# Inverse of the DeltaNet chunk matrix: masks applied to the decay factors, the diagonal written ahead of the row operations, one group of 64-row matmuls queued later

## Chip, cores and metric

The kernel runs on one core of one Trainium2 chip. The metric is the device time of one execution in microseconds, taken as the median of several runs. A core has TensorE (PE, with weight loads listed apart as PEld), VectorE (DVE), ScalarE (ACT), GpSimd (POOL) and SyncE (SP). Each works through its own queue in order. DMAs are started from the queues of SP and ACT here, and an engine that has to start a DMA waits at that place of its queue until the DMA's input is ready.

## What is computed

The reference is one layer of a hybrid decoder with 512 tokens, 16 meta tokens and a width of 2048: one input projection, three token mixers side by side (gated DeltaNet with 6 heads, gated linear attention (GLA) with 5, forgetting attention with 5), gates, and one output projection. The change concerns the DeltaNet mixer. In chunks it solves a unit lower triangular system for each head:

```
decay = exp(where(causal, g[..., :, None] - g[..., None, :], -inf))
a_mat = where(strict, einsum('bhncd,bhnsd->bhncs', kb, kc) * decay, 0.0)
sol   = triangular_solve(eye + a_mat, rhs, lower=True, unit_diagonal=True)
```

The kernel uses chunks of 128 tokens (and one of the 16 meta tokens) and computes the inverse of `eye + a_mat` explicitly.

## The kernel before

**The projection carries the time line.** The input projection is a long run of matmuls (line 174, tile `pp`): 128x128 weight blocks in two parts each (`whi` and `wlo`, so that the product is nearly exact) against the normalised input. A weight half of 128x1024 is loaded by SP, rounded to `whi` by ACT (L144), and the rest `wlo` is formed by DVE (L145). There are two buffers of each, so the cast of a half waits until PE has done with the half before the last one. A head's columns take 48 matmuls of 512 columns or 96 of about 264. Everything else (DeltaNet, GLA, attention) is put in between these matmuls by a scheduler that orders each engine's queue when the program is built. The list `order` holds the projection's matmuls as they are traced. `behind(mm, n)` makes a matmul follow the n-th projection matmul traced after that point; with `PM = (308,310)` it holds back the first 32-row matmul of each group's inverse.

**DeltaNet runs in two groups of three heads.** For a group, `dn_keys` makes the keys (projection, convolution, SiLU), then for the meta tokens and for each of the four 128-token blocks: the transposed keys `pk`, the key products `pg` (L433), the decay differences `e2` on DVE (L434) clamped at zero from below, their exponential on ACT (L435), and the product `an = pg * scale * e2` on DVE (L438). Below the diagonal `an` holds the negated matrix; on and above the diagonal it holds other finite values, because the clamp makes the decay factor 1 there. A POOL select (L412) is already in use for another tile of the same shape, `at`.

`dn_inverse` then works in four steps.

1. The 32x32 diagonal blocks of `an` (48 of them, and three 16x16 of the meta tokens) are written to DRAM (`scr`, L449, and `scmeta`, L453) and read back as 51 rows of 1024 (`ab`, L454 and L455), all from ACT's queue. `ab` is zeroed first by POOL (L446).
2. Thirty pairs of DVE operations (L463 and L465) turn each row into the inverse by row operations. They stand in DVE's queue between weight splits and evacuations.
3. Two POOL selects (L466 and L468) put zeros above the diagonal and ones on it. Then `ab` goes to DRAM (`sc`, L471) and comes back as `xc` and `xm` (L474, L476, tiles `iv` and `xm`). DVE transposes them (L478, L479).
4. From the 32-row inverses come the 64-row and 128-row ones: matmuls `pm` (L485), ACT copies (L489), matmuls `pl` (L494, L495), an ACT copy (L496), copies into `uf` (ACT L502, DVE L504), and for each half q the matmuls `pn` (L515), an ACT copy (L517), matmuls `pu` (L520) and a DVE copy (L521). `uf` is zeroed by POOL (L499).

`dn_mix` then runs the recurrence with `uf`. The order in which the parts are traced is: keys, values, queries, inverse, mixing of group 0, the same for group 1, then the GLA gates (`gz`, `stgz`, `zsgz`), GLA pairs (`gk`, ...), and attention. SiLU takes a maximum on POOL (L294), three ACT steps (L295 to L297) and a product on DVE (L298).

Of the kernel before, what the change touches and what calls it, by code (L numbers as in the profile page):

```python
# [14 lines left out]
ALU = mybir.AluOpType  # L15
# [12 lines left out]
H = 3  # L28
# [49 lines left out]
def tile_hybrid_trunk(ctx, tc, xT, xtok, mtok, w_gate, w_in, w_out, consts, lmask, fin_w, out, dbg=None):  # L78
# [20 lines left out]
    V, A, G, PE = nc.vector, nc.scalar, nc.gpsimd, nc.tensor  # L99
# [62 lines left out]
    def behind(mm, n):  # L162

        later.append((mm.ins, len(order) + n))
# [85 lines left out]
    for b in range(5):  # L250
        r = NM if b == 4 else P
# [9 lines left out]
    for b in range(5):  # L261
        r = NM if b == 4 else P
# [55 lines left out]
    for k in range(KT):  # L318
        for xx in (xh, xl):
            for a in range(2):  # L320
                PE.matmul(pgate[a][:, :HT], wg[k // 8][:, k % 8, :], xx[k][:, a * HT : (a + 1) * HT],
                          start=(k == 0 and xx is xh), stop=(k == KT - 1 and xx is xl))
# [35 lines left out]
    def conv_silu(key, blk, dst, meta=True):  # L358

        t0 = 0 if meta else NM  # L360
        pb = row(f"pb{blk}")
        if meta:
            G.memset(pb[:, 0:3], 0.0)
        evac(inproj(key, first=0 if meta else NM - 4), pb, off=3)
        c = row(f"cv{blk}")[:, t0:T]
        V.tensor_scalar_mul(c, pb[:, t0:T], cwc[:, blk, 0:1])
        for w in range(1, 4):
            V.scalar_tensor_tensor(out=c, in0=pb[:, t0 + w : w + T], scalar=cwc[:, blk, w : w + 1], in1=c,  # L368
                                   op0=ALU.mult, op1=ALU.add)
        silu(dst[:, t0:], c, f"c{blk}")  # L370
# [4 lines left out]
    def dn_keys(g):  # L375

        st = {}
        hs = range(H * g, H * g + H)
        kT = six.tile([P, H, T], F32, tag="six", name=f"kT{g}")
        for j, h in enumerate(hs):  # L380
            conv_silu(("dk", h), 6 + h, kT[:, j])
        gb = six.tile([P, H, T], F32, tag="six", name=f"gb{g}")
        nc.scalar.dma_start(out=gb, in_=gd[6 + H * g : 6 + H * g + H, :].partition_broadcast(P))
        kd = six.tile([P, NN, P], F32, tag="six", name=f"kd{g}")
        at = six.tile([P, NN, P], F32, tag="six", name=f"at{g}")
        an = six.tile([P, NN, P], F32, tag="six", name=f"an{g}")
        sk = wk.tile([P, 5, H], F32, tag="sk", name=f"sk{g}")
        kdm = t15(f"kdm{g}", (NM, H, P))
        anm = wk.tile([NM, H, NM], F32, tag="anm", bufs=1, name=f"anm{g}")
        atm = wk.tile([NM, H, NM], F32, tag="atm", bufs=1, name=f"atm{g}")  # L390
        cols = wk.tile([P, 4, 5, H], F32, tag="cols", name=f"cols{g}")
        nb2, br, nbg, tmp = (cols[:, i] for i in range(4))
        gcl = lambda b, j: gcol[:NM if b == 4 else P, b, 6 + H * g + j : 6 + H * g + j + 1]
        G.memset(sk, 1.0)
        for b in (4, 0, 1, 2, 3):
            r = NM if b == 4 else P
            ts = slice(0, NM) if b == 4 else bsl(b)
            pk = psm.tile([P, 512], F32, tag="m", name=f"pk{g}{b}")
            for j in range(H):
                PE.transpose(pk[:r, j * P : (j + 1) * P], kT[:, j, ts], ident)  # L400
            for j in range(H):
                sq = wk.tile([P, P], BF16, tag="sq", name=f"sqk{g}{b}{j}")
                A.activation(sq[:r], pk[:r, j * P : (j + 1) * P], AF.Square, accum_out=sk[:r, b, j : j + 1])
            e = at[:, b * H : b * H + H, :] if b < 4 else atm
            for j in range(H):
                V.tensor_scalar(e[:r, j, :], gb[:r, j, ts], gcl(b, j), 0.0, ALU.subtract, ALU.min)
            A.activation(e, e, AF.Exp)
            for j in range(H):
                dst = kd[:, b * H + j, :] if b < 4 else kdm[:, j, :]
                V.tensor_scalar_mul(dst, pk[:r, j * P : (j + 1) * P], e[:r, j, r - 1 : r])  # L410
            if b < 4:
                G.affine_select(out=e, in_=e, pattern=[[0, H], [1, P]], base=0, channel_multiplier=-1,  # L412
                                compare_op=ALU.is_ge, fill=0.0)
        A.activation(tmp, sk, AF.Ln, bias=eps_c)
        A.activation(br, tmp, AF.Exp, scale=-0.5)
        lb = gcol[:, :, H * g : H * g + H]
        gg = gcol[:, :, 6 + H * g : 6 + H * g + H]
        for sl, r in ((slice(0, 4), P), (slice(4, 5), NM)):
            c = lambda t: t[:r, sl, :]
            A.activation(c(tmp), c(lb), AF.Exp)  # L420
            V.tensor_tensor(out=c(nb2), in0=c(tmp), in1=c(br), op=ALU.mult)
            V.scalar_tensor_tensor(out=c(tmp), in0=c(nb2), scalar=-1.0, in1=c(br), op0=ALU.mult, op1=ALU.mult)
            V.tensor_copy(c(br), c(nb2))
            V.tensor_copy(c(nb2), c(tmp))
            A.activation(c(nbg), c(gg), AF.Exp)
            V.tensor_tensor(out=c(nbg), in0=c(nbg), in1=c(nb2), op=ALU.mult)
        for b in (4, 0, 1, 2, 3):
            r = NM if b == 4 else P
            ts = slice(0, NM) if b == 4 else bsl(b)
            pg = psm.tile([P, 512], F32, tag="m", name=f"pg{g}{b}")  # L430
            e2 = t15(f"e2{g}{b}")
            for j in range(H):
                PE.matmul(pg[:r, j * r : (j + 1) * r], kT[:, j, ts], kT[:, j, ts], start=True, stop=True)  # L433
                V.tensor_scalar(e2[:r, j, :r], gb[:r, j, ts], gcl(b, j), 0.0, ALU.subtract, ALU.max)  # L434
            A.activation(e2[:r, :, :r], e2[:r, :, :r], AF.Exp, scale=-1.0)  # L435
            for j in range(H):
                dst = an[:, b * H + j, :] if b < 4 else anm[:, j, :]
                V.scalar_tensor_tensor(out=dst, in0=pg[:r, j * r : (j + 1) * r], scalar=nb2[:r, b, j : j + 1],  # L438
                                       in1=e2[:r, j, :r], op0=ALU.mult, op1=ALU.mult)
        st.update(kT=kT, kd=kd, at=at, an=an, kdm=kdm, anm=anm, br=br, nbg=nbg)  # L440
        return st

    def dn_inverse(g, st):
        an, anm = st["an"], st["anm"]
        ab = six.tile([NN * 4 + H, 1024], F32, tag="six", name=f"ab{g}")
        G.memset(ab, 0.0)  # L446
        scr = drp.tile([NN * 4, 1024], F32, tag="scr", name=f"scr{g}", bufs=2)
        for r in range(4):
            nc.scalar.dma_start(  # L449
                out=scr.rearrange("(n r) (a c) -> r a n c", r=4, a=32)[r],  # L450
                in_=an[32 * r : 32 * r + 32, :, 32 * r : 32 * r + 32])
# [3 lines left out]
        nc.scalar.dma_start(  # L455
            out=ab[NN * 4 : NN * 4 + H, :].rearrange("h (a c) -> h a c", a=32)[:, 0:NM, 0:NM],
            in_=scm_.rearrange("a h c -> h a c"))
        a3 = ab.rearrange("p (a c) -> p a c", a=32)
        for j in range(1, 31):
            m = 31 - j  # L460
# [2 lines left out]
            V.tensor_tensor(out=t3, in0=a3[:, j + 1 :, j : j + 1].to_broadcast([NN * 4 + H, m, j]),  # L463
                            in1=a3[:, j : j + 1, 0:j].to_broadcast([NN * 4 + H, m, j]), op=ALU.mult)
            V.tensor_tensor(out=a3[:, j + 1 :, 0:j], in0=a3[:, j + 1 :, 0:j], in1=t3, op=ALU.add)  # L465
        G.affine_select(out=a3, in_=a3, pattern=[[1, 32], [-1, 32]], base=0, channel_multiplier=0,  # L466
                        compare_op=ALU.is_gt, fill=0.0)
        G.affine_select(out=a3, in_=a3, pattern=[[1, 32], [-1, 32]], base=0, channel_multiplier=0,  # L468
                        compare_op=ALU.not_equal, fill=1.0)
        sc2 = drp.tile([NN * 4 + H, 1024], F32, tag="sc2", name=f"sc2{g}", bufs=2)  # L470
        nc.scalar.dma_start(out=sc2, in_=ab)  # L471
        iv = six.tile([P, 4, NN, 32], F32, tag="six", name=f"iv{g}")
# [9 lines left out]
        for n in range(NN):  # L482
            for q in range(2):
                lo_, hi_ = slice(64 * q, 64 * q + 32), slice(64 * q + 32, 64 * q + 64)
                mm = PE.matmul(pm[lo_, n, :], an[hi_, n, lo_], uc[hi_, n, :], start=True, stop=True)  # L485
# [12 lines left out]
        uf = six.tile([P, NN, P], F32, tag="six", name=f"uf{g}")  # L498
# [6 lines left out]
        for q in range(2):  # L505
            ns = range(q * 6, q * 6 + 6)
            nsl = slice(q * 6, q * 6 + 6)
            b64 = t15(f"b64{g}{q}", (64, 6, 64))
            G.memset(b64, 0.0)
            V.tensor_copy(b64[0:32, :, 0:32], xc[0:32, nsl])  # L510
            V.tensor_copy(b64[32:64, :, 32:64], xc[32:64, nsl])
            V.tensor_copy(b64[32:64, :, 0:32], l1[32:64, nsl])
            pn = psm.tile([64, 6, 64], F32, tag="m", name=f"pn{g}{q}")
            for n in ns:
                PE.matmul(pn[:, n - q * 6, :], an[64:128, n, 0:64], uf[64:128, n, 64:128], start=True, stop=True)  # L515
            m2 = t15(f"m2{g}{q}", (64, 6, 64))
            A.copy(m2, pn)  # L517
            pu = psm.tile([64, 6, 64], F32, tag="m", name=f"pu{g}{q}")
            for n in ns:
                PE.matmul(pu[:, n - q * 6, :], b64[:, n - q * 6, :], m2[:, n - q * 6, :], start=True, stop=True)  # L520
            V.tensor_copy(uf[0:64, q * 6 : q * 6 + 6, 64:128], pu)  # L521
# [362 lines left out]
    PM = (308,310)  # L884
# [85 lines left out]
    for cc in range(4):  # L970
# [7 lines left out]
        n = (FIRST // 2, KT // 2, KT // 2, LAST // 2)[cc]  # L978
# [27 lines left out]
    for tb in range(4):  # L1006
# [9 lines left out]
        r = rr[:, tb : tb + 1]  # L1016
# [67 lines left out]
```

## Time and profile before

| what | value |
|---|---|
| runs | 1031.01, 1032.09, 1033.81 us; median 1032.09 |
| profiled execution | 1035.39 us, span 1033.7 us, mean granted TensorE clock 0.992 |
| PE busy | 1011.4 us, 7799 matmuls |
| row operations L463 / L465 | 60 each, 20.1 / 21.4 us |
| selects L466 / L468 | 2 each, mean 1258 / 1404 ns |
| selects L412 (128x384) | 8, mean 1175 ns |
| `sc` to `iv`, issue to issue | 208.49 to 215.15 us in group 0, 392.80 to 399.48 us in group 1 |

"Busy" counts an engine's instructions as they run; a wait in the list of waits is time in which the engine's queue stood still until the named instruction of another engine was done. The granted clock is the share of TensorE's full clock in a stretch. A line of the timeline gives the start in us from the span's start, the duration, engine, line, operation, tile written and tiles read, sizes, and how many instructions were merged; in brackets the idle time ahead of it and what ended it.

### The profile page before, as it was taken

To read this page: it belongs to the slowest core of one execution; us is meant where nothing else is said; L and a number is where in the kernel's file an instruction comes from. 1 tells how busy PE (TensorE), PEld (TensorE's weight loads), DVE (VectorE), ACT (ScalarE), POOL (GpSimd) and SP (SyncE) were. 2 spreads that over 40 slices of the span, in tenths; PEclk is the share of its full clock that TensorE was granted. 3 is DMA by queue.
4 is the path that set the end of the run, shared out by engine and by line. 5 is a ranking of instruction groups with operands and counts; after the bars stand their busy time and mean duration, and the time that the engine had idled before them with its cause. 6 is when DMAs were issued, how large, how long until landed. Compare 5 with 4: busy or idle time off the path is not lost.

```text
span 1033.7 us, 19032 instructions
## 1 busy us (share of the span) xinstructions
PE 1011.4 (98%) x7799; PEld 910.3 (88%) x7799; DVE 566.7 (55%) x1240; ACT 411.7 (40%) x899; POOL 136.4 (13%) x137
## 2 busy tenths in 40 slices
PE   9999999999999998999989999999999999999996
PEld 7899999989999888899989879898998988888885
DVE  6366868856577883243747474445454574423234
ACT  6644533343455343243444444343333353213223
POOL 0022212221122222100101010110101010000014
PEclk9999999999999998999999999999999999999998
DMA  9613232323222233132112122222232254222244
GB/s 354 239 62 115 83 90 91 102 78 108 78 83 81 78 102 99 49 94 74 62 48 83 44 92 66 91 82 92 82 93 82 93 193 133 82 100 85 102 142 163
DMA packets 42347, 105.15 MB, mean 102 GB/s; under 512 B 10589, under 2 KB 13917, under 8 KB 42260
## 3 DMA queue, kind: packets, MB, share of 16 engines
q1 hardware_dynamic: 28000, 92.33, 26.3%
q10 hardware_dynamic: 14260, 11.61, 4.1%
q8 instruction: 61, 1.00, 0.4%
q14 instruction: 26, 0.21, 0.1%
HBM read 98.74 MB, written 5.05 MB: 100 GB/s over the span
## 4 chain that ended last, share of the span: by engine, by line
PE 66%; DVE 5%; DMA 3%; issue 3%; ACT 2%; POOL 1%; ACTq 0%; POOLq 0%; DVEq 0%
PE pp L174 39%; PE pa L932 15%; DMA sc<-ab 1%; PE pss L717 1%; POOL stgz L294 1%; DVE wlo L145 1%; PE pfo L877 1%; PE pfa L845 1%; PE py L593 1%; PE pb L932 1%; PE pfx L860 1%; DVE ab L465 1%; PE po L608 1%; PE po L607 1%; PE pa L570 0%
## 5 line engine op out<-in xcount | busy, mean ns | idle before, releaser
L174 PE MATMUL pp<-xh,whi 128*128 128x264 f32 (+2 forms) x1456 | 378.2, 311 | 0.8 <-DVE vg L285 0.5
L174 PE MATMUL pp<-xl,whi 128*128 128x264 f32 (+2 forms) x1456 | 378.2, 311 | 0.0
L174 PE MATMUL pp<-xh,wlo 128*128 128x264 f32 (+2 forms) x1456 | 376.5, 310 | 0.0
L174 PEld LDWEIGHTS pp<-xh,whi 128*128 128x128 f32 x1456 | 244.4, 189 | 16.8 <-issue 3.1
L174 PEld LDWEIGHTS pp<-xl,whi 128*128 128x128 f32 x1456 | 245.6, 190 | 14.0 <-issue 1.0
L174 PEld LDWEIGHTS pp<-xh,wlo 128*128 128x128 f32 x1456 | 245.2, 190 | 13.1 <-issue 0.2
L145 DVE TENSOR_TENSOR wlo<-raw,whi 128x1024 fp32r<-128x1024 f32 x110 | 137.1, 1246 | 112.0 <-ACT whi L144 110.4
L144 ACT CAST whi<-raw 128x1024 fp32r<-128x1024 f32 x110 | 115.4, 1049 | 202.3 <-PE pp L174 175.3
L932 PE MATMUL pa<-wloo,oh 128*128 128x512 f32 x224 | 88.0, 393 | 0.0
L932 PE MATMUL pa<-whio,ol 128*128 128x512 f32 x224 | 87.9, 393 | 0.0
L932 PE MATMUL pa<-whio,oh 128*128 128x512 f32 x224 | 78.3, 396 | 0.0
L145 DVE TENSOR_TENSOR wloo<-rawo,whio 128x1024 fp32r<-128x1024 f32 x29 | 35.8, 1236 | 76.4 <-ACT whio L144 76.3
L144 ACT CAST whio<-rawo 128x1024 fp32r<-128x1024 f32 x29 | 30.4, 1049 | 83.8 <-PE pa L932 56.8
L932 PEld LDWEIGHTS pa<-whio,ol 128*128 128x128 f32 x224 | 42.2, 188 | 9.7
L932 PEld LDWEIGHTS pa<-wloo,oh 128*128 128x128 f32 x224 | 42.1, 188 | 9.4
L932 PEld LDWEIGHTS pa<-whio,oh 128*128 128x128 f32 x224 | 41.9, 188 | 9.2
L294 POOL TENSOR_SCALAR stc<-cv 128x528 f32<-128x528 f32 (+1 forms) x18 | 28.1, 1562 | 164.5 <-DVE cv L368 164.5
L368 DVE SCALAR_TENSOR_TENSOR cv<-pb,cpk,cv 128x528 f32<-128x528 f32 (+1 forms) x54 | 40.8, 756 | 0.8
L959 POOL TENSOR_TENSOR acc<-acc,fw 128x512 f32<-128x512 f32 x12 | 15.7, 1348 | 158.6 <-DMA fw<-in_fin_w 158.6
L285 DVE TENSOR_TENSOR pb<-pp,rstd 128x264 f32<-128x264 f32 (+1 forms) x36 | 13.8, 423 | 16.0 <-PE pp L174 15.9
L465 DVE TENSOR_TENSOR ab<-ab,ot 51x30 f32<-51x30 f32 (+14 forms) x60 | 21.4, 357 | 1.4
L463 DVE TENSOR_TENSOR ot<-ab 51x30 f32<-51x30 f32 (+14 forms) x60 | 20.1, 334 | 3.1 <-DMA ab<-scmeta 1.5
(384 smaller groups left out, 1279.8 us busy)
## 6 DMA issues: line engine op xcount, KB each, us to landing
raw<-in_w_in SPq DMA_DIRECT2D x110, 512.0 KB, 3.3
rawo<-in_w_out SPq DMA_DIRECT2D x29, 512.0 KB, 3.3
xt<-in_xtok SPq DMA_DIRECT2D x8, 512.0 KB, 9.9
acc<-in_xtok ACTq DMA_DIRECT2D x16, 256.0 KB, 5.2
out<-acc SPq DMA_DIRECT2D x16, 256.0 KB, 3.0
xs<-in_xT SPq DMA_DIRECT2D x7, 528.0 KB, 6.5
gb<-gd ACTq DMA_DIRECT2D x2, 792.0 KB, 7.4
eg<-gd ACTq DMA_DIRECT2D x8, 192.0 KB, 3.7
```

Of the source, the lines that this page charges most:

```text
L144: A.copy(hi, raw)
L145: V.tensor_tensor(out=lo, in0=raw, in1=hi.bitcast(F32), op=ALU.subtract)
L174: mm = PE.matmul(p_[:, :nt], wt[:, j * m : (j + 1) * m], xx[k][:, t0 : t0 + nt], start=(k == 0 and wt is hi and xx is xh), stop=(k == KT - ...
L285: V.tensor_tensor(out=o, in0=p_[rows], in1=rstd[rows, t0 : t0 + n], op=ALU.mult)
L294: G.tensor_scalar_max(t, src, LOW)
L368: V.scalar_tensor_tensor(out=c, in0=pb[:, t0 + w : w + T], scalar=cwc[:, blk, w : w + 1], in1=c, op0=ALU.mult, op1=ALU.add)
L463: V.tensor_tensor(out=t3, in0=a3[:, j + 1 :, j : j + 1].to_broadcast([NN * 4 + H, m, j]), in1=a3[:, j : j + 1, 0:j].to_broadcast([NN * 4 + ...
L465: V.tensor_tensor(out=a3[:, j + 1 :, 0:j], in0=a3[:, j + 1 :, 0:j], in1=t3, op=ALU.add)
L593: PE.matmul(py[:, j * P : (j + 1) * P], uf[:, b * H + j, :], z[:, j, :], start=True, stop=True)
L607: PE.matmul(pj, at[:, b * H + j, :], y[:, j, :], start=True, stop=False)
L932: PE.matmul(p_, o_[:, s], w_, start=(first and n == 0), stop=(last and n == 2), **kw)
L959: G.tensor_tensor(out=acc[tb, cc], in0=acc[tb, cc], in1=fw[cc], op=ALU.mult)
```

## The change

Zeros are made where the decay factors are made: a POOL select on `e2` after each exponential keeps only what is strictly below the diagonal, five per group. The diagonal of `ab` is set to one by a POOL memset behind the reads into `ab` and ahead of the row operations. The two selects behind the row operations go. In group 0 the first `pn` matmul gets a place of its own: behind projection matmul `PM[0] + 72` = 380.

```
             A.activation(e2[:r, :, :r], e2[:r, :, :r], AF.Exp, scale=-1.0)
+            G.affine_select(out=e2[:r, :, :r], in_=e2[:r, :, :r], pattern=[[0, H], [-1, r]], base=0,
+                            channel_multiplier=1, compare_op=ALU.is_gt, fill=0.0)
...
             in_=scm_.rearrange("a h c -> h a c"))
+        G.memset(ab[:, 0:1024:33], 1.0)
         a3 = ab.rearrange("p (a c) -> p a c", a=32)
...
-        G.affine_select(out=a3, in_=a3, pattern=[[1, 32], [-1, 32]], base=0, channel_multiplier=0,
-                        compare_op=ALU.is_gt, fill=0.0)
-        G.affine_select(out=a3, in_=a3, pattern=[[1, 32], [-1, 32]], base=0, channel_multiplier=0,
-                        compare_op=ALU.not_equal, fill=1.0)
...
-                PE.matmul(pn[:, n - q * 6, :], an[64:128, n, 0:64], uf[64:128, n, 64:128], start=True, stop=True)
+                mm = PE.matmul(pn[:, n - q * 6, :], an[64:128, n, 0:64], uf[64:128, n, 64:128],
+                               start=True, stop=True)
+                if g + n == 0:
+                    behind(mm, PM[g] + 72)
```

The scheduler orders every queue anew for the changed program, so instructions around these places move as well. In the built order, `pm` of group 0 keeps its place among the projection matmuls; `pn` of group 0 moves from 59 to 72 projection matmuls behind the first `pm`; `pm` of group 1 stands 71 instead of 79 matmuls behind the start of the first GLA key block; and the ACT and DVE queues between the two groups are interleaved differently.

## Prediction

> **What bounds the kernel now.** I read the page first.
>
> ```profile
> PE 1011.4 (98%) x7799; PEld 910.3 (88%) x7799; DVE 566.7 (55%) x1240; ACT 411.7 (40%) x899; POOL 136.4 (13%) x137
> ...
> PEclk9999999999999998999999999999999999999998
> ```
>
> TensorE is the bound; the time falls only where PE waits or runs at a lower clock. So I read PE's own waits next (total us, times, longest).
>
> ```profile
> PE pss L717 <- issue: 3.5, 3, 1.4
> PE pm L485 <- DVE iv L479: 3.0, 1, 3.0
> PE pn L515 <- DVE uf L504: 2.3, 1, 2.3
> ```
>
> Of 15 us of waiting, 5.35 belong to the inverse: pn (the 64-row matmuls) of group 0 at 229.9 to 232.2, and pm (the 32-row ones) of group 1 at 400.2 to 403.2. What follows such a wait is in the table by windows (stretch, its length, PE busy, granted clock, DMA share, GB/s).
>
> ```profile
> 228.00:232.00 4.00, 1.87 (x16) 1.00 0.02 6
> 232.00:234.00 2.00, 1.80 (x15) 0.68 0.04 8
> 234.00:236.00 2.00, 2.00 (x11) 0.50 0.68 193
> 236.00:238.00 2.00, 2.00 (x19) 0.96 0.17 70
> 400.00:403.20 3.20, 0.21 (x2) 1.00 0.42 68
> 403.20:405.00 1.80, 1.77 (x50) 0.56 0.00 0
> 405.00:407.00 2.00, 2.00 (x11) 0.50 0.44 133
> 407.00:409.00 2.00, 2.00 (x10) 0.50 0.32 129
> 409.00:410.40 1.40, 1.40 (x5) 0.56 0.00 0
> ```
>
> After each wait the clock halves. PE counts as busy there, but does less. Lost work is length times (1 - clock): 0.64+1.00+0.08 = 1.72 us after pn, 0.79+1.00+1.00+0.62 = 3.41 us after pm. So the two waits cost 2.33+1.72 = 4.05 and 3.02+3.41 = 6.43 us, **10.48 us** together. Between 5 and 1025 us I found no other dip. What releases pm in group 1 is a chain across POOL, the ACT queue and DVE:
>
> ```profile
> 390.18 1.26 POOL L466 TENSOR_SCALAR_AFFINE_SELECT ab<-ab 51x1024 f32<-51x1024 f32 x1 [6.08 <-DVE ab L465]
> 391.51 1.26 POOL L468 TENSOR_SCALAR_AFFINE_SELECT ab<-ab 51x1024 f32<-51x1024 f32 x1
> ```
> ```profile
> 392.80 0.26 ACTq L471 DMA_DIRECT2D sc<-ab  x1
> ...
> 399.48 0.38 ACTq L474 DMA_DIRECT2D iv<-sc  x1
> ...
> 403.26 2.07 ACT L502 COPY uf<-iv 32x384 f32<-32x384 f32 x4 [0.37 <-DVE iv L479]
> 405.36 0.96 ACT L489 COPY iv<-pm 32x384 f32<-32x384 f32 x2
> ```
>
> Last row operation 390.1, two selects, write to DRAM issued 392.8, read back issued 399.5, landed by 402.4 (the tile's rows give 2.9 and 4.5 us to landing), transposed on DVE, then pm.
>
> **The change, part by part.** *Selects out.* Two selects leave each chain: 392.80-390.10 = 2.7 us in group 1, 208.49-205.45 = 3.0 in group 0. *Ones ahead.* A 51x32 memset now stands between the landing of ab and the first row operation. No row shows one that small; 128x3 memsets take 0.10 and 51x1024 ones 0.95. I take 0.15 (nearest: the small one). In group 0 DVE waits for PE later in the chain (0.32 at 172.1, 0.63 at 183.4), which absorbs it; in group 1 nothing does.
>
> *Masks.* Ten POOL selects are added (eight 128x384, two 16-row). L412 is the same shape: 0.52 beside PSUM reads, 3.44 at worst, mean 1.18. In group 0 three of them come ahead of a SiLU max (L294 at 121.5); at 0.5 to 0.7 each the value v comes 1.5 to 2 us later. The PE transposes of v start at 130.24, v is ready at 127.1, so 3.1 us of cover: cost 0; at the mean of 1.18 it is 3.5, cost 0.4; at 3.44 it is rival 3. In group 1 the product `an` depends on the mask, and the scheduler also puts the last pg four matmuls later and two an products behind a weight split (2 x 0.28): the chain starts about 0.6 us later. One row operation moves into a wait for ACT (-0.3). Last row operation: 390.1+0.3 = 390.4.
>
> *pn of group 0.* It stood 24+35 = 59 projection matmuls behind pm and now stands 72 behind: 13 x 0.122 = 1.6 us later on PE, with nothing added.
>
> Now each group in the order in which the changed program issues. **Group 0:** write issued 205.5, landing 6.64 later as before: 212.15; read landed 2.9 to 4.5 later: 215.1 to 216.7; transposed 0.58 later. pm is reached at 220.3: no wait. But ACT's read issue now precedes a weight cast, and DVE's transposes precede the weight split for the half that PE begins at 217.5. The split ends at 217.5 or 219.1, and PE wants it at 218.0: 0 to 1.1 us; I take 0, since the read at 212.15 has no weight load beside it, like the 2.9 us one. On ACT follow four copies, a SiLU, a cast, two copies of pm, a SiLU (it waits for DVE and POOL until 225.9 or 227.5), the copy of pl at 228.5 or 230.1, then DVE's copies: pn can go at 229.3 or 230.9. PE reaches it at 225.2 + 48 x 0.122 = 231.1. **Wait gone, and the clock with it: -4.05.** Without the move PE would be there at 229.5, so the shorter chain does most of this and the 13 places are its cover.
>
> **Group 1** (times as if PE had not gained before): write 390.4, landed 397.1, read landed 400.0, transposed 400.6. PE reaches pm eight matmuls earlier than before (71 instead of 79 behind the start of the gk block at 390.47): 390.47 + 71 x 0.122 = 399.15. It waits 1.5 us; 3.1 if the read takes 4.5. Then pl: it needs ACT's copies of pm, which now stand behind the four copies (2.10), two SiLU steps (2 x 0.66), a cast (0.96) and take 0.96 themselves: 5.3 us behind the transposes. PE is at pl after pm (0.87) and 24 projections (3.05): 3.9 us behind. So a second wait of 1.3 us appears where there was none, because PE no longer runs at half clock there. Waits 2.8 instead of 3.02.
>
> Whether 1.5 and 1.3 us halve the clock decides the rest. At 522.96 PE waits 1.35, and its windows stay at 1.00; 2.33 halved it. 1.5 is nearest to the first: no drop, and 3.41 saved. [...]
>
> **Sum:** 4.05 + (6.43 - 2.8) = 7.7 us. Against the profiled execution (span 1033.7, execution 1035.39): 1027.7. That execution lies 3.3 us above the median shown, 1032.09. If the 3.3 is a constant of profiling, the median becomes 1024.4; if it is clock loss that other executions met less of, 1027.7. I take the middle, **1026.0 us**.
>
> **Rivals.**
> 1. *The clock still halves in group 1.* For: 1.5 us lies between 1.35 and 2.33, and pm uses 32 rows only. Against: the wait is half of the old one. It adds 1.7 (the loss after pn) to 3.4 (after pm): 1027.7 to 1029.4.
> 2. *The read lands late and takes the place of the selects.* 4.5 us instead of 2.9 in both groups: pm waits 3.1 (+1.6), the clock halves (+3.4), the split in group 0 is 1.1 late: 1026.0+6.1 = 1032.1, no change. For: group 0 had 4.5. Against: a weight load ran beside that one.
> 3. *Slower: the masks starve on POOL.* One select took 3.44 us beside DVE operations on SBUF. If the three ahead of the SiLU in group 0 all do, v comes 10.3 late, less 3.1 of cover: PE waits 7.2 us and loses 1.7 to 3.4 in clock. Group 1's chain starts up to 7 late as well. Together about +17 on 1026.0: 1043. It decides from about 2 us a select ((3.1 + 3.0)/3, where both groups' waits eat the gain). [...]
> 4. *Group 1 is clean too* (chain 3 us earlier than I count): 1026.0-2.8 = 1023.2.
>
> That the change doesn't do what it says is weak: the built order has no L466/L468 selects, and pn stands 72 behind.
>
> **How the numbers follow.** Forecast 0.60, rival 1 0.14, rival 2 0.12, rival 3 0.06, rival 4 0.08. 0.3% (3.1 us) is about what a measurement of this kernel can tell from no change: faster means under 1029.0, slower over 1035.2. Faster: 0.60+0.08+0.09 of rival 1 = 0.77. Same: 0.05 of rival 1 and rival 2 = 0.17. Slower: 0.06. The range reaches from below rival 4, 1022.5, over rival 1 into rival 2, 1031.0; rival 3 and most of rival 2 are left out.
>
> **What would show it.** PE's waits list pn no more; windows near 230 to 238 stay at 1.00; pm and pl of group 1 show about 1.5 and 1.3, clock 1.00 after them; L294 near 121.5 starts up to 2 us later without a PE wait at L534. A PE wait at L174 near 218 speaks for rival 2; mask selects of 2 us and more for rival 3. I am wrong if new waits arise in the mixing stage (240 to 320), whose order the scheduler redrew and which I took at its old cost, zero wait.

## Result, and the profile after

| | before | changed |
|---|---|---|
| median | 1033.1 us (7 runs) | 1027.94 us (7 runs, 1026.89 to 1031.36) |
| ratio | | 0.9954, interval 0.9941 to 0.9967 |
| profiled execution | 1035.39 us | 1027.62 us |
| its span, mean granted clock | 1033.7 us, 0.992 | 1025.9 us, 0.998 |

The changed kernel is faster by 5.2 us between the medians and by 7.8 us between the two profiled executions. The prediction was 1026.0 us (1022.5 to 1031.0), with 7.7 us between the profiled executions. Line numbers are two or three higher behind the added mask, one lower behind the removed selects and two higher again behind the edit at `pn` (the mask is L436, `pm` L484, `pl` L493, `pn` L514).

The page of the changed kernel, first part and the clock in 40 slices:

```profile
PE 1007.7 (98%) x7799; PEld 907.0 (88%) x7799; DVE 565.3 (55%) x1240; ACT 412.5 (40%) x899; POOL 134.3 (13%) x145
...
PEclk9999999999999999999999999999999999999999
```

PE still sets the time. It counts 3.7 us less busy with the same 7799 matmuls, which fits the half-clock stretches being gone: matmuls of 264 columns took PE 0.22 us each there (two start at 405.39 us in before, the next two at 405.83) and 0.12 us at full clock (397.74, 397.98), and all of it counts as busy. PE's waits (us in total, times, longest):

```profile
PE pm L484 <- DVE iv L478: 0.8, 1, 0.8
PE pl L493 <- ACT iv L488: 0.8, 2, 0.5
```

`pn` is no longer listed. `pm` fell from 3.0 to 0.8, and `pl`, which was not listed before, waits 0.8. The stretches where the clock had fallen (stretch, length, PE busy, clock, DMA share, GB/s):

```profile
228.00:232.00 4.00, 4.00 (x35) 1.00 0.00 0
232.00:234.00 2.00, 2.00 (x22) 1.00 0.80 258
234.00:236.00 2.00, 2.00 (x18) 1.00 0.03 12
396.00:399.00 3.00, 2.15 (x59) 1.00 0.00 0
399.00:402.00 3.00, 2.45 (x22) 1.00 0.00 0
402.00:405.00 3.00, 2.79 (x101) 1.00 0.57 180
```

The first three rows have no idle time at all. The last three have 1.6 us of it, and the clock stays at 1.00. The timeline of ACT and its queue in group 1 (start, duration, instruction):

```profile
387.15 0.26 ACTq L470 DMA_DIRECT2D sc<-ab  x1
393.50 0.38 ACTq L473 DMA_DIRECT2D iv<-sc  x1
...
397.10 2.07 ACT L501 COPY uf<-iv 32x384 f32<-32x384 f32 x4
...
401.21 0.95 ACT L488 COPY iv<-pm 32x384 f32<-32x384 f32 x2
```

The write goes out at 387.15, directly behind the last row operation (ended 387.12): the selects' 2.7 us are gone. The read follows 6.35 us later (6.68 before). The copies of `pm`, which `pl` needs, stand in ACT's queue behind the four copies into `uf`, a SiLU step, a weight cast and another SiLU step.

**Two numbers for each execution.** Each execution has a span and a mean clock. Span times (1 - clock) is what the lowered clock took away over the whole span; the remainder is the rest of the span. As means over runs on one chip (the changed kernel ran there as `e8_after_again`):

| | runs | lost to the clock | rest |
|---|---|---|---|
| before | 11 | 5.4 us | 1027.3 us |
| changed | 6 | 2.9 us | 1024.4 us |
| difference | | -2.4 us | -2.9 us |

So about half of the gain is clock, and half is the rest of the span, which holds the waits. The clock is given to three digits, a step of 1 us for one execution, and by the scatter of the runs each difference is good to some 0.4 to 0.7 us.

The profiled execution of before lost 1033.7 x 0.008 = 8.3 us by this measure, more than the mean of before in any of three sets of runs (5.8, 6.0 and 5.4 us). Not all of it cost time. In that execution PE's last matmul ends at 1025.4 us, and the clock falls behind it, while the outputs are still being written:

```profile
1028.04:1033.68 5.64, 0.00 (x0) 0.50 0.71 252
```

That is 2.8 us of the 8.3. Over the 13 profiles kept this tail is 1.3 to 3.6 us, with a mean of 2.5 in the four with the old chain and 2.5 in the seven with the short chain and `pm` not put earlier, so it drops out of the difference but not out of the single numbers. Where PE still had matmuls to run, the profiled execution of before lost 5.1 us and that of the changed kernel none.

### The profile page after: what moved, and what is told of

Its sections match the earlier page's. It is cut to its first block, busy times and chain, and to the rows that moved or that the text cites. A ratio compares the mean times of both kernels' runs of the same rounds, so it can differ in the third digit from the quotient of the medians.

```text
span 1025.9 us, 19045 instructions
## 1 busy us (share of the span) xinstructions
PE 1007.7 (98%) x7799; PEld 907.0 (88%) x7799; DVE 565.3 (55%) x1240; ACT 412.5 (40%) x899; POOL 134.3 (13%) x145
## 4 chain that ended last, share of the span: by engine, by line
PE 87%; DVE 5%; ACT 2%; DMA 2%; issue 1%; POOL 1%; ACTq 0%; SPq 0%; DVEq 0%; POOLq 0%
PE pp L174 54%; PE pa L934 16%; PE pp L227 4%; POOL stgz L294 1%; PE pss L719 1%; DVE wlo L145 1%; PE pgate L321 1%; PE pfo L879 1%; PE pfa L847 1%; DMA sc<-ab 1%; DVE ab L468 1%; PE pg L433 1%; PE py L595 1%; PE pb L934 1%; PE pfx L862 1%
## 5 line engine op out<-in xcount | busy, mean ns | idle before, releaser
L145 DVE TENSOR_TENSOR wlo<-raw,whi 128x1024 fp32r<-128x1024 f32 x110 | 135.0, 1227 | 105.8 <-ACT whi L144 104.1
L145 DVE TENSOR_TENSOR wloo<-rawo,whio 128x1024 fp32r<-128x1024 f32 x29 | 35.9, 1236 | 77.0 <-ACT whio L144 76.9
L368 DVE SCALAR_TENSOR_TENSOR cv<-pb,cpk,cv 128x528 f32<-128x528 f32 (+1 forms) x54 | 41.4, 767 | 0.7
```

Source lines behind the costliest of these rows:

```text
L145: V.tensor_tensor(out=lo, in0=raw, in1=hi.bitcast(F32), op=ALU.subtract)
```

## The experiments

Behind the expectations stand three theories. **A**: the gain is the waits plus the half clock behind them, and the shorter chain brings most of it. **W**: only the waits cost. **POOL**: the added masks cost something of their own. Each text says under its own names what it expects. Each run is told against the kernel before on the same chip.

**Parts alone.** `e1_no_move` is the changed kernel without the later place of `pn`:

```
...
-                if g + n == 0:
-                    behind(mm, PM[g] + 72)
```

> The changed kernel without the later place of pn in group 0 (pn stands 59 instead of 72 projection matmuls behind pm). Theory (shorter chain does it): in the changed kernel DVE had pn's last input ready at 229.5 us, and PE would be there at about 230.4 with 59 places, so pn waits under 0.3 us, the clock stays at 1.00 near 232 to 238, and the time is that of the changed kernel, 1027.9 within 1 us. Rival (the move does it): pn waits 1 us or more, with a halved clock behind it, and the time is 2 to 4 us longer, 1030 to 1032.

Measured: ratio 0.9961 (0.9947 to 0.9975), median 1029.80 us against 1034.32. That is 1.9 us over the 1027.9 that I expected to meet within 1 us, in a set in which the kernel before was 1.2 us over the 1033.1 of the result. `pn` does not wait here either, and the windows from 228 to 236 us stay at 1.00 without idle time. The shorter chain alone removes the wait in group 0. What the move adds to it is not resolved (0.9961 against 0.9954).

`e2_move_only` is the kernel before with that edit alone:

```
...
+                if g + n == 0:
+                    behind(mm, PM[g] + 72)
```

> The kernel before with the later place of pn alone; masks and selects as before. Theory: PE reaches pn 1.6 us later, so its wait falls from 2.3 to about 0.7 us, too short to halve the clock; 1.6 and up to 1.7 us of clock go, group 1 keeps its wait of 3 us: 1029.8 to 1031.5 by the median. Rival (waits alone count, the clock dip belongs to something else): only the place changes, the dip near 232 to 236 stays, 1031.5 to 1033.

Measured: ratio 0.9983 (0.9973 to 0.9993), 1.8 us. `pn` waits 0.8 in place of 2.3 us and the clock near 230 us no longer falls. Group 1 is as it was, with 3.4 us at `pm` and this behind it (windows of PE):

```profile
401.00:403.00 2.00, 1.76 (x51) 0.73 0.00 0
403.00:405.00 2.00, 2.00 (x11) 0.50 0.38 121
405.00:407.00 2.00, 2.00 (x12) 0.91 0.35 141
```

The median of 1032.04 us lies above my range and inside the rival's, but against the 1034.32 us of before in the same set it is 2.3 us shorter, and the dip that the rival wanted to stay is gone. So move and shorter chain are two ways to the same gain in group 0; only the shorter chain reaches group 1. By the profiles the move took away 1.5 us of wait and 1.7 us of clock, 3.2 us in all; the runs show 1.8 us of it (0.7 to 2.8 by the interval).

`e6_masks_kept` is the kernel before with the masks added and the old selects left in:

```
+            G.affine_select(out=e2[:r, :, :r], in_=e2[:r, :, :r], pattern=[[0, H], [-1, r]], base=0,
+                            channel_multiplier=1, compare_op=ALU.is_gt, fill=0.0)
```

> The kernel before with the five masks a group added and the two selects behind the row operations kept, so that only the masks' own cost shows. Theory: POOL has room, no PE wait at the transposes of v (L534 region near 130 us); in group 1 the chain starts about 0.6 us later and pm waits as much longer: 1033 to 1034.5. Rival (masks starve on POOL): selects of 2 us and more, a PE wait near 130 us, 1036 or more.

Measured: ratio 1.0002 (0.9991 to 1.0014), no wait at the transposes of v. So the ten masks cost less than about 1.4 us. The 0.6 us more at `pm` did not show: it waited 2.9 us, but in this execution the read-back of group 1 was issued 5.25 us behind the write where before had 6.68, which hides a delay of that size. `e7_masks_g0_twice` makes each mask twice in group 0 of the changed kernel:

```
+            if g == 0:
+                G.affine_select(out=e2[:r, :, :r], in_=e2[:r, :, :r], pattern=[[0, H], [-1, r]], base=0,
+                                channel_multiplier=1, compare_op=ALU.is_gt, fill=0.0)
```

> The changed kernel with the new mask on the decay factors made twice in the first group (the second one changes no value), so that POOL has five more selects there, some 4 us in the burst ahead of v's multiplication by its gate at 123.5 us. In the changed kernel v was done at 127.5 us and PE reached v's transposes at 131.35 us. Theory A (PE is covered up to about 3.8 us of POOL's work): v is done at about 131.7 us, PE waits 0.5 to 1 us there, no clock dip, time within 1 us of the changed kernel, ratio to the kernel before 0.995 to 0.9965. Rival of starving (the cover is less than that, since a select beside VectorE takes up to 1.4 us where one alone takes 0.52): PE waits 2 us or more at v's transposes, the clock halves, 4 us or more over the changed kernel, ratio over 0.998.

Measured: ratio 0.9953 (0.9932 to 0.9975), the same as the changed kernel. POOL's timeline there, with the second selects on L439:

```profile
118.35 2.45 POOL L436 TENSOR_SCALAR_AFFINE_SELECT e<-e 128x384 f32<-128x384 f32 x1 [0.80 <-ACT e L435]
120.87 0.52 POOL L439 TENSOR_SCALAR_AFFINE_SELECT e<-e 128x384 f32<-128x384 f32 x1
121.34 1.47 POOL L436 TENSOR_SCALAR_AFFINE_SELECT e<-e 128x384 f32<-128x384 f32 x2
122.77 1.00 POOL L439 TENSOR_SCALAR_AFFINE_SELECT e<-e 128x384 f32<-128x384 f32 x2
...
124.23 1.52 POOL L294 TENSOR_SCALAR stc<-cv 128x528 f32<-128x528 f32 x1
```

The gate of v begins at 124.23, 0.7 us later than in the changed kernel (123.49) and not 4 us as I had expected: the added selects took 0.5 us each, and the first selects took 2.45 and 1.47 for two where the changed kernel has 4.18 for three. v was done at 129.1 us and PE reached its transposes at 130.8, so 1.7 us of cover were left. The expectation's 127.5 us for v in the changed kernel is the end of its last SiLU step on ACT (126.86 + 0.65); the product on DVE, which makes v, ended at 128.9, so the cover there was 2.4 us and not 3.8. The expectation's 0.52 us is not that of a select alone either: in the changed kernel VectorE was at work beside the select of 0.52 us at 115.34 (L410, 115.08 to 117.48) as beside the three of 4.18 us (L434, L368, L145 and others). This run did not use up the cover. It shows only that double masks cost nothing; how much POOL work PE would stand there stays open.

**How long may PE wait?** `e5_after_pm1_294` and `e5_after_pm1_286` move `pm` of group 1 forward by 16 and 22 matmuls in the changed kernel, which gives PE its wait back without the selects (the first is shown, the second has 286):

```
-    PM = (308,310)
+    PM = (308,294)
```

> The changed kernel with the second group's inverse matmuls put 16 projection matmuls earlier (308,294), so that the wait at pm becomes 0.8 + 1.95 = 2.8 us, about what it was before the change. Theory A (a wait of over about 2 us halves the clock behind it, and the change gained by that as well as by the wait): granted clock 0.5 to 0.75 within 8 us behind pm in the profile, time lost to the clock 1.7 to 3.4 us more than in the changed kernel, 3.6 to 5.4 us over it in all, ratio to the kernel before 0.999 to 1.0006. Theory W (only the wait costs; the clock is halved by something else that the change took away, or after a longer idle stretch only): no dip behind pm, 2 us over the changed kernel, ratio 0.997 to 0.9975.

> The changed kernel with the second group's inverse matmuls put 22 projection matmuls earlier (308,286), so that the wait at pm becomes 0.8 + 2.7 = 3.5 us, with 30 matmuls between pm and pl in place of 24, so that pl no longer waits. Theory A: a dip to half the clock behind pm in every run, 3.4 to 6.8 us lost to it; together with the wait (2.7 longer, 0.8 saved at pl) 5.3 to 8.7 us over the changed kernel, ratio to the kernel before 1.000 to 1.004. [...]

Measured: 1035.89 us, ratio 1.0012 (0.9993 to 1.0032), and 1035.8 us, ratio 1.001 (0.9993 to 1.0026): more than A's size for the first, within A's for the second. The whole gain is gone. The waits at `pm` were 3.4 and 3.6 us, and both profiles have the clock at 0.50 behind them. For 294 (windows of PE):

```profile
398.00:400.00 2.00, 0.51 (x32) 1.00 0.09 13
400.00:402.00 2.00, 2.00 (x37) 0.72 0.03 8
402.00:404.00 2.00, 2.00 (x11) 0.50 0.00 0
```

On average span times (1 - clock) was 6.0 and 5.7 us, against 2.9 to 3.4 in the runs of the changed kernel and its near copies (4.3 in `e1_no_move`). That only the wait costs, the first form of W, falls. Its second form, a fall behind a longer idle stretch only, these two runs cannot tell from A, since the wait of 294 came out at 3.4 us and not at 2.8; falls of the clock behind shorter waits (2.3 and 3.0 us in before, 1.45 and 2.0 us in runs below) exclude it. A was too low for 294 in part because two waits came with it that I had not counted: 1.0 and 1.8 us in the mixing steps, at 434 and 444 us, the second with a dip of its own in the profile of 294. Placing one matmul earlier moved what the projection covered later on.

**Can the rest be had by a later place?** `e3_before_pm1_340` is the kernel before with `pm` of group 1 moved back by 22 matmuls:

```
-    PM = (308,310)
+    PM = (308,340)
```

> The kernel before with pm of group 1 held back to the 340th projection matmul instead of the 310th (22 matmuls later in the built queue, about 3.2 us of PE time); nothing is taken out of the chain. Theory (a wait costs itself and the clock behind it): pm's wait of 3.0 goes, no half clock from 403 to 410, 4 to 6.4 us shorter: 1026.7 to 1029. Rival (the wait alone counts): 3 us shorter at most, 1030, with the clock still at 0.5 after 403. Rival (the chain, not the place, is what PE waits for): no change, since another wait takes its place at pl.

Measured: ratio 1.0006 (0.9996 to 1.0016), so nothing, though the wait and the dip behind `pm` are gone. PE's waits tell a part of it:

```profile
PE pp L174 <- DVE wlo L145: 1.3, 1, 1.3
...
PE pq L572 <- ACT sqq L574: 1.1, 1, 1.1
```

I compared the starts of equal PE, DVE and ACT instructions in the two traces. This execution began 1.0 us late at 391 us. At 417 us the weight casts, which follow PE's projection, stood 4.2 us ahead, but the copies of the inverse stood 0.9 to 2.4 us late: part of that lead is only PE work put off. At 471 us, behind the mixing steps, 0.75 us of it was left, a gain of 1.8 us. From 391 to 471 us PE idles 3.3 us in both executions: the wait of 3.0 us at `pm` came back as 1.3 us at a weight split queued behind the transposes, 1.1 at `pq`, 0.4 at `py` and 0.5 at `psn`. What is won there is the clock's part, 1.8 of 3.4 us; the other 1.6 us I could not place. Behind 535 us the execution was 0.5 us late, by a clock dip at 526 to 532 us (0.88, 0.50, 0.76 in windows of 2 us) in a stretch of short GLA matmuls where PE idles in both kernels. Here a faster PE met consumers that were no earlier.

`e4_after_pm1_326` does the same to the changed kernel, by 16 matmuls:

```
-    PM = (308,310)
+    PM = (308,326)
```

> The changed kernel with one number more changed: the second group's inverse matmuls are put 16 projection matmuls later (308,326 in place of 308,310), about 1.95 us at 0.122 us a matmul. Theory A (what is left in the second group is the waits of 0.8 us at pm and 0.8 us at pl, nothing else): both go, 1.6 us saved, ratio to the kernel before 0.9939 where the changed kernel had 0.9954. Theory B (the room behind the inverse is used up: the run on the kernel before with pm 22 matmuls later won its wait and its clock back and lost all of it again to a weight split of 1.3 us behind the transposes, to waits of 2 us in the mixing and to a clock dip at 525 us): the waits at pm and pl go, but new ones of 0.5 to 2 us show at pq, psn or a split between 400 and 475 us, ratio 0.995 to 0.998.

Measured: ratio 0.9955 (0.9937 to 0.9973), no gain. The wait moved. A projection matmul of PE, and the windows behind it:

```profile
401.91 0.79 PE L174 MATMUL pp<-xh,whi 128*128 128x512 f32 x1 [1.45 <-ACT whi L144]
```
```profile
400.00:402.00 2.00, 0.55 (x5) 0.98 0.00 0
402.00:404.00 2.00, 1.96 (x4) 0.50 0.00 0
404.00:406.00 2.00, 2.00 (x7) 0.67 0.80 262
```

PE now reaches the next weight half before ACT has cast it. In ACT's queue that cast (400.83) stands behind the four copies into `uf` (398.20 to 400.27) and a SiLU step. The same four copies stand ahead of the copies of `pm` that `pl` waits for in the changed kernel. So the last runs move them to VectorE, which has nothing to do from 397.6 to 400.8 us in the changed kernel:

```
-            A.copy(uf[s, :, s], uc[s])
+            V.tensor_copy(uf[s, :, s], uc[s])
```

> The changed kernel itself, unchanged, to stand beside the two that follow. Ratio to the kernel before 0.994 to 0.997; in the profile waits of 0.3 to 1.1 us at pm and 0.8 us at pl, none at pn.

> The changed kernel with the four copies of the inverse blocks into uf on VectorE in place of ScalarE. In the changed kernel the second group's four copies held ScalarE from 397.10 to 399.17 us, and a SiLU step, a weight cast, another step and only then the copies of pm (401.21 to 402.16) stood behind them, for which PE waited 0.8 us at pl. Theory A (it is ScalarE's queue that pl waits for): three SiLU steps, the cast and the copies of pm follow one another from 396.5 us, 1.9 + 1.05 + 0.95, so pm's copies end at about 400.4, PE gets to pl at 401.2 and doesn't wait; the split of the weights on VectorE begins at 399.9 in place of 400.81, behind the four copies (some 1.5 us); 0.8 to 1.0 us saved, no new wait. Rival: VectorE's four copies hold up the split that PE needs next, and a wait at the projection matmuls takes the place of the one at pl; nothing saved.

> The same, and the second group's inverse matmuls 16 projection matmuls later (308,326), as in the run that gained nothing by that because PE then waited 1.45 us for a weight cast that stood on ScalarE behind the four copies, with half the clock behind it. Theory A (the copies on ScalarE were the cause of that wait): the cast ends 1.8 us earlier, no wait over 0.3 us at the cast and none at pm and pl, no clock dip between 395 and 410 us, 1.6 us saved over the changed kernel. Rival (the room behind the inverse is used up whichever engine copies): a wait of about 1 us remains at the cast or at the split, or comes back in the mixing steps up to 475 us, and nothing is saved.

| run | median | ratio (interval) | lost to the clock, rest (means) |
|---|---|---|---|
| `e8_after_again` | 1028.96 us | 0.9951 (0.9935 to 0.9967) | 2.9, 1024.4 us |
| `e9_uf_on_dve` | 1027.04 us | 0.9939 (0.9917 to 0.9960) | 3.3, 1022.7 us |
| `e9_uf_on_dve_326` | 1026.91 us | 0.9935 (0.9919 to 0.9950) | 2.7, 1022.9 us |

In both runs with the copies on VectorE, `pl` waits no more. ACT in `e9_uf_on_dve_326`:

```profile
398.52 1.04 ACT L144 CAST whi<-raw 128x1024 fp32r<-128x1024 f32 x1
399.46 0.96 ACT L488 COPY iv<-pm 32x384 f32<-32x384 f32 x2
```

The first cast comes 1.2 us and the copies of `pm` 1.75 us earlier than in the first profile of the changed kernel (399.74 and 401.21). PE's wait of 1.45 us for the cast is replaced by one of 0.6 us for a split, between the 0.3 us of theory A and the 1 us of the rival; `pm` and `pl` are not listed, and the windows from 396 to 412 us stay at 1.00. In `e9_uf_on_dve` the copies of `pm` end at 401.1 us and the clock stays at 1.00 as well, but PE waits 1.5 us at `pm`. Theory A holds for the queue. In time, the rest of the span falls by 1.5 to 1.7 us, where 0.8 to 1.0 and 1.6 were expected; with some 0.5 us of uncertainty, and with the intervals of the three ratios overlapping, the gain over the changed kernel is not shown by the times alone. Against the kernel before, the two medians are 7.6 and 7.7 us shorter.

The repeated profile of the changed kernel held something else. PE's wait and the windows there:

```profile
PE pm L484 <- DVE iv L478: 2.0, 1, 2.0
```
```profile
400.00:402.00 2.00, 2.00 (x13) 0.62 0.00 0
402.00:404.00 2.00, 2.00 (x11) 0.53 0.00 0
```

The same program waited 2.0 us where its first profile had 0.8, more than the 1.1 that I had allowed, and here the clock fell. The 0.8 us expected at `pl` did not come: at half clock PE reached `pl` later. The read was issued 7.33 us behind the write instead of 6.35. Over the profiles of all variants with the short chain that gap was 5.8 to 7.6 us in group 1, and 4.92 to 4.95 us in group 0. What makes it differ in group 1 no run shows.

## Why the prediction was right, and where it was off

- **Selects out, ones ahead.** Right. The last row operation ended at 387.12. My 390.4 was counted as if PE had not gained earlier; less the 4.05 us of group 0, and with the 1.0 us by which this execution lay behind from its first stage on (a wait of 1.0 us at L227, 0.2 before), it gives 387.35. The memset took 0.15 us as forecast.
- **Masks.** Right at 0. Three of them took 4.18 us (1.39 each, more than I assumed; the longest of the ten took 2.54 us). v was ready at 128.9 us and PE came to its transposes at 131.35, so 2.4 us of the 3.1 us of cover were left. `e6_masks_kept` prices all ten at nothing within about 1.4 us. Rival 3 fell.
- **Group 0.** Right: no wait, no dip; `e1_no_move` shows that the chain does it and the move is cover. Two inner numbers were off in the good direction: the read was issued 4.93 and not 6.64 us after the write, and the split for the half that PE wants at 218 us was done in time. So the selects are not all of it. The transposes ended 4.4 us earlier than before (215.88 for 220.25), 5.4 with the 1.0 us by which this execution began late: 3.0 are the selects, 1.7 the shorter gap between write and read, and the rest a shorter way from the read to the transposes. The gap is 6.66 us in all four profiles with the old chain; no run separates what shortened it from the selects' going. In group 1 nearly all of the gain of the chain is the selects' 2.7 us: from the write's issue to the end of the transposes it took 10.4 us before and 9.9 us in the changed kernel. Rival 2 fell in this profile: the read landed 3.0 us after its issue in both groups.
- **Group 1.** Right in mechanism. `pm` waited 0.8 (0.5 in `e1_no_move`, 2.0 in `e8_after_again`) for my 1.5; `pl` waited 0.8 for my 1.3, for the reason given: `e9_uf_on_dve` moved the four copies and the wait went. "No drop, and 3.41 saved" holds in the first profile of the change and in `e1_no_move`, not in `e8_after_again`. So rival 1 is what some executions do, beside the forecast in others. The rule behind that choice, that 1.5 us is nearer to 1.35 than to 2.33, was too weak: a wait of 1.53 us kept the clock (`e9_uf_on_dve`) and one of 1.45 us lost it (`e4_after_pm1_326`). That it came out right in the first profile is partly luck.
- **The sum and the frame.** Between the profiled executions 7.7 us were forecast and 7.8 came. The clock's part was 1.72 + 3.41 = 5.13 us in the forecast, and 5.1 us in the two profiles. In waits the forecast was 2.33 + 3.02 - 2.8 = 2.55 us; 5.35 - 1.6 = 3.7 us came, and about 1 us of it was lost again by the late start, so that the sums agree so closely is luck. As means over runs the clock's part is only 2.4 us and the rest 2.9. **For the median, the mis-sized term is the clock**: the forecast took it from one profile of before, which by span times (1 - clock) had met 8.3 us where its runs have 5.4 to 6.0 on average.
- **The step that failed** is "I take the middle": half of the 3.3 us by which the profiled execution lay above the median was taken for a constant of profiling. The profiled execution of the changed kernel lies 0.3 us below its median, so there is no such constant in sight. The second reading, that others met less clock loss, gave 1027.7 us, within 0.3 of the measured median. It is not the whole of it: 1032.09 us was the median of three runs, and the later medians of the kernel before are 1033.1 to 1034.65 us, so that the profiled execution lies only 0.7 to 2.3 us above them.

## What to carry to other kernels

Price a wait of TensorE with the clock behind it (1.72 us behind 2.33 and 3.41 us behind 3.02 in the profile of before), but take the clock's part from several executions, and leave out what falls behind the last matmul: one profile shows one draw. After a chain is shortened, look at which queue its next consumer stands in; here the next limit was four copies on ScalarE that could go to an idle VectorE. Moving a wait's matmul later only helps if what it uncovers (the next cast, the mixing steps) is ready earlier too.

## What the runs showed of the hardware

- **As long as PE had matmuls to run, half clock came in pieces of 3.4 us here.** From the windows, the half-clock stretch of `e8_after_again` runs from 402 - 2 x 0.76 = 400.48 to 402 + 2 x 0.94 = 403.88 us, that of `e4_after_pm1_326` from 401.92 to 405.32: 3.40 us each, 1.7 us lost. Behind `pm` in before it is twice that (403.42 to 410.23). The clock came back at 236.16 and at 410.23 us in before, 174.07 us apart. Of pieces of 3.40 us that is nearest to 51, and 174.07 / 51 makes a piece 3.413 us, an estimate of mine from these two times.
- **What went ahead of a fall in these profiles is a piece in which PE did little, not a wait of some length.** In the 3.41 us ahead of the dip of `e4_after_pm1_326`, PE idled 1.45 us and ran `pm` and projection matmuls in the rest. A wait of 1.53 us (`e9_uf_on_dve`) and waits of 0.8 and 0.8 us did not halve the clock; 1.45, 2.01, 2.3 and more did. The falls and recoveries of one execution lie on one grid of 3.413 us: in `e8_after_again` the fall at 400.46 and the one behind the last matmul at 1025.10 are 183.0 pieces apart. I laid this grid over all 13 profiles, from 15 us to PE's last matmul, and left out the pieces at half clock. The clock falls 13 times, and in the piece ahead of each fall PE is busy for 0.39 to 1.97 us. In all other pieces but one it is busy for 2.02 us or more. In before it is 0.39 and 1.08 us ahead of the two falls and 2.15 us or more elsewhere; in the first profile of the changed kernel it is 2.18 us or more and the clock does not fall. The exception is 1.60 us in `e5_after_pm1_286` at 440.15, where the clock stayed; so busy time tells most of it and not all. Two of these pieces, that of `e8_after_again` (the clock fell at its end) and that of `e9_uf_on_dve` (it did not):

```profile
397.05:400.46 3.41, 1.74 (x55) 1.00 0.13 19
396.72:400.13 3.41, 2.17 (x58) 1.00 0.01 1
```

The wait of 1.53 us in `e9_uf_on_dve` began at 396.43, so the grid cut it and 1.24 us of it lie in this piece; the one of 1.45 us in `e4_after_pm1_326` lies in one piece whole. The grid does not stand at the same place in each execution: the fall at 1022.53 in the first profile of the changed kernel is 182.25 pieces from the 400.46 of `e8_after_again`, the same program. That fits a wait of 1.45 us costing clock in one execution and one of 1.53 us none in another.

- **The same pn wait of 2.3 us** cost 1.72 us of clock in before and 3.4 us in `e6_masks_kept` (windows of 2 us from 233 us: 0.62, 0.50, 0.50, 0.68).
